# Eight feed-forward gate products as seven block products each

## The chip, the cores and the metric

The kernel runs on one core of a Trainium2 chip. TensorE (PE) multiplies, VectorE (DVE) and ScalarE (ACT) work on tiles in SBUF and PSUM, GpSimd (POOL) and SyncE (SP) issue transfers here. The metric is the device time of one execution in microseconds (us); lower is better. A matmul or tile shape such as 128x512 is partitions by elements.

## The reference

One decoder layer on x (256 tokens, 2048 wide), everything in f32:

```
h = swiglu(rms_norm(x), wg1, wu1, wd1);   x = x + 0.5 * rms_norm(h)
m = hybrid_mixer(rms_norm(x), mem, ...);  x = x + rms_norm(m)
h = swiglu(rms_norm(x), wg2, wu2, wd2);   out = x + 0.5 * rms_norm(h)
swiglu(u) = (silu(u @ wg) * (u @ wu)) @ wd        wg, wu: 2048 x 5504
```

The mixer projects u, runs a gated recurrence, a forgetting attention and an attention over a memory (mem_kv = rms_norm(mem) @ w_mem_kv, which needs nothing of x), gates the three and multiplies by w_o. Every norm has its gains.

## The kernel before, in words

**Products in halves.** Each f32 operand is split exactly into a high and a low part of 12 bits (`split`: the copy on ScalarE, L164, then the subtraction on VectorE, L165), and a product is three matmuls into the same sum: high by high (L278), high by low (L279), low by high (L281). The weights are the moving operand, 512 columns at a time; the input, transposed, is the stationary one, 128 x 128.

**Weights.** `Weights` loads the k tiles (128 rows) of up to 1024 columns: a raw tile of 1 MB (two k tiles, `N_RAW` 3) comes on SP's queue, and each k tile is split into a pair whi, wlo of 1024 wide (`N_SPLIT` 6 pairs).

**`linear`** walks over k in batches and lets the two token tiles t = 0, 1 of 128 tokens alternate within a batch; `head` and `tail` are the lengths of the first and the last batch. Its callbacks take what is in PSUM: `evac` per token tile, `by_chunk` after each 512 columns. `before` runs ahead of a batch. Work that needs TensorE in between (transposes) is put off by a batch (`soon`, `tasks`). PSUM has 5 banks for sums and 3 for transposes.

**`ffn`.** d_ff is 43 tiles of 128, in parts of 16, 16 and 11. In a part, each eight tiles make a gate group (16 k tiles x 2 token tiles x 2 chunks x 3 = 192 matmuls; silu at L391 on ScalarE) and an up group (192 matmuls; L396 on VectorE multiplies by the gate), then hT is transposed and split. Behind a part comes its down product; its sum is kept in SBUF tiles y.

**`closer`** ends a sub-layer: y is multiplied by the gains (L343), normalised with the residual added (L360, on VectorE, token tile by token tile), transposed into the next input (L171, L182, L183) and stored. The row scale rstd of that input is applied later, where sums leave PSUM.

**Order.** Every engine has an in-order queue, which the Tile scheduler sets from its own model of times; buffers come from pools (`slot` 21, `tmp` 7), so an operation also waits for a free buffer. Memory keys and values are made behind the first feed-forward; the transposes of the memory stand among the batches of its last down product. At the start x is loaded, transposed and split ahead of the batches of the first gate group.

```
for f in range(f0, f1, 8):                     # in each of the three parts
    linear(from_uT(u), Weights(KD, chunks(wg)), evac_gate)
    linear(from_uT(u), Weights(KD, chunks(wu)), evac_up)
```

Of the kernel before, what the change touches and what calls it, by code (L numbers as in the profile page):

```python
# [9 lines left out]
F32 = mybir.dt.float32  # L10
# [17 lines left out]
N_SLOT = 21  # L28
N_TMP = 7
N_RAW = 3  # L30
N_SPLIT = 6
N_ACC = 5
N_TP = 3
BIG = 6


def constants():
    """Identity, causal bias and the level masks: they depend on shapes alone."""
# [15 lines left out]
def layer(ctx: ExitStack, tc: tile.TileContext, a, out: bass.AP):  # L54
# [22 lines left out]

    def acc(w):
        return psp.tile([P, 512], F32, tag="acc", bufs=N_ACC, name=nm("acc"))[:, :w]

    def tp(*shape):
        n = int(np.prod(shape))
        t = psp.tile([P, 512], F32, tag="tp", bufs=N_TP, name=nm("tp"))[:, :n]
        if len(shape) == 2:
            t = t.rearrange("p (a b) -> p a b", b=shape[1])
        return t
# [12 lines left out]
    def columns(rows, q):  # L99
        """Vectors [1, n * 128] as n columns each, found by col()."""  # L100
# [16 lines left out]
    turn_first = columns([("ffn1_pre", 16)], S)  # L117
    turn_rest = columns([("mem_norm", 16), ("mix_pre", 16), ("ffn2_pre", 16), ("hgrn_lb", 12), ("hgrn_gnorm", 6)], G)
# [35 lines left out]
    def touch(func, src):  # L154
        """Has the table of func loaded by the time src is there."""
# [6 lines left out]
    def split(hi, lo, src):  # L162
        """hi + lo = src exactly, 12 bits each."""
# [3 lines left out]
    def transposed(src, n):  # L167
        """n blocks of [P, 128] of src, each transposed, in PSUM."""
# [5 lines left out]
    def split_T(hi, lo, src, n, gain=None):  # L174
        """hi, lo: [P, n, 128] slices for src^T (times gain per row)."""
# [10 lines left out]
    class Weights:  # L186
# [3 lines left out]
        def __init__(self, nk, chunks, kb=None, early=0):  # L190
# [6 lines left out]
            self.kb = kb or max(1, 2048 // self.width)  # L197
# [6 lines left out]
        def load(self, n):  # L204
            width, k0 = self.width, len(self.parts)
            raw = pool.tile([P, 2048], F32, tag="raw", bufs=N_RAW, name=nm("raw"))[:, :n * width]
# [742 lines left out]
```

## Time and profile before

| | |
|---|---|
| device time, median of 3 runs | 2263.7 us (2262.32 to 2264.56) |
| span of the profiled execution | 2262.2 us |
| TensorE busy | 2243.5 us (99%), 10674 instructions |
| VectorE busy | 1245.6 us (55%) |
| ScalarE busy | 1048.0 us (46%) |
| loaded and stored | 434.33 MB, mean 192 GB/s |

The profile is of one execution, and its span lies 1.5 us below the median of the runs. Busy time is the time an engine spent in instructions; a row of a group gives the count, the busy time and the mean of one, then how long the engine was idle just before them and what ended that. The chain goes back from the last instruction to what each waited for.

### The profile page before, as it was taken

The page shows a single profiled execution, that of the slowest core. Times are in us where ns is not written, and L with a number is a line of the kernel's source. Part 1 is how long each engine was busy: PE and PEld are TensorE (multiplying, and loading weights), DVE is VectorE, ACT ScalarE, POOL GpSimd, SP SyncE. Part 2 cuts the span into 40 slices and gives each one's busy share as a digit, 9 for nine tenths or more (in the row PEclk, how much of TensorE's full clock was granted, in tenths as well). Part 3 has the DMA queues.
Part 4 walks back from the last instruction along what each step waited for, and adds up shares of the span by engine and source line. Part 5 has one row for each costly group of instructions (what it writes and reads, how often), then busy time and mean ns, then how long its engine had stood idle before and what let it go on. Part 6 is the DMA issues. An engine that isn't in the chain of part 4 may idle for free.

```text
span 2262.2 us, 26732 instructions
## 1 busy us (share of the span) xinstructions
PE 2243.5 (99%) x10674; PEld 1914.7 (85%) x10674; DVE 1245.6 (55%) x1519; ACT 1048.0 (46%) x1351; POOL 33.1 (1%) x61
## 2 busy tenths in 40 slices
PE   9999999999999999999999999999999999999998
PEld 7888888888898799999888888888888888888896
DVE  5545445454456856686555545557545445455455
ACT  6444444443446744445444444446444444443443
POOL 0000000000000000000000000000000000000000
PEclk9999999999999999999999999999999999999999
DMA  8555565557555644546656566665656555557553
GB/s 267 187 191 189 178 206 187 201 172 258 188 182 197 224 154 154 166 151 176 194 179 199 187 197 216 217 208 188 203 187 186 187 202 186 186 192 255 179 184 121
DMA packets 138540, 434.33 MB, mean 192 GB/s; under 512 B 9080, under 2 KB 42064, under 8 KB 138416
## 3 DMA queue, kind: packets, MB, share of 16 engines
q1 hardware_dynamic: 133568, 417.41, 55.6%
q0 software_dynamic: 4672, 15.15, 2.4%
q8 instruction: 83, 1.36, 0.2%
q14 instruction: 41, 0.34, 0.0%
q10 hardware_dynamic: 176, 0.07, 0.0%
HBM read 426.30 MB, written 6.30 MB: 191 GB/s over the span
## 4 chain that ended last, share of the span: by engine, by line
PE 97%; DMA 1%; DVE 1%; ACT 0%; SPq 0%; issue 0%; DVEq 0%; ACTq 0%
PE acc L278 31%; PE acc L279 31%; PE acc L281 31%; PE tp L171 2%; PE tp L671 1%; DMA x<-in_x_dram 0%; DMA raw<-in_ffn_wu_dram 0%; DMA x<-in_mem_dram 0%; DVE y L360 0%; DVE wlo L165 0%; ACT whi L164 0%; PE tp L584 0%; PE tp L600 0%; ACT junk L160 0%; PE tp L665 0%; PE tp L818 0%
## 5 line engine op out<-in xcount | busy, mean ns | idle before, releaser
L165 DVE TENSOR_TENSOR wlo<-raw,whi 128x1024 fp32r<-128x1024 f32 (+2 forms) x818 | 958.5, 1177 | 866.0 <-ACT whi L164 829.1
L164 ACT ACTIVATE whi<-raw 128x1024 fp32r<-128x1024 f32 (+2 forms) x818 | 833.2, 1024 | 1006.6 <-PE acc L281 956.4
L278 PE MATMUL acc<-whi,uh 128*128 128x512 f32 (+1 forms) x2264 | 856.6, 379 | 1.6 <-ACT uh L182 1.5
L279 PE MATMUL acc<-wlo,uh 128*128 128x512 f32 (+1 forms) x2264 | 849.2, 376 | 0.8 <-DVE wlo L165 0.8
L281 PE MATMUL acc<-whi,ul 128*128 128x512 f32 (+1 forms) x2264 | 670.2, 376 | 0.1
L278 PEld LDWEIGHTS acc<-whi,uh 128*128 128x128 f32 x2264 | 425.0, 188 | 68.2 <-ACT uh L182 3.0
L279 PEld LDWEIGHTS acc<-wlo,uh 128*128 128x128 f32 x2264 | 425.2, 188 | 66.5 <-DVE wlo L165 1.3
L281 PEld LDWEIGHTS acc<-whi,ul 128*128 128x128 f32 x2264 | 421.1, 188 | 66.6 <-DVE ul L183 0.5
L278 PE MATMUL acc<-whi,hh 128*128 128x512 f32 x688 | 269.2, 391 | 0.0
L279 PE MATMUL acc<-wlo,hh 128*128 128x512 f32 x688 | 268.0, 390 | 0.0
L281 PE MATMUL acc<-whi,hl 128*128 128x512 f32 x688 | 228.4, 389 | 0.0
L281 PEld LDWEIGHTS acc<-whi,hl 128*128 128x128 f32 x688 | 129.1, 188 | 26.9
L278 PEld LDWEIGHTS acc<-whi,hh 128*128 128x128 f32 x688 | 129.2, 188 | 26.5
L279 PEld LDWEIGHTS acc<-wlo,hh 128*128 128x128 f32 x688 | 129.2, 188 | 26.3
L396 DVE SCALAR_TENSOR_TENSOR sg<-acc,rstd,sg 128x512 f32<-128x512 f32 (+1 forms) x44 | 31.2, 733 | 34.3 <-PE acc L281 29.9
L278 PE MATMUL acc<-whi,eh 128*128 128x512 f32 x128 | 50.1, 391 | 0.0
L279 PE MATMUL acc<-wlo,eh 128*128 128x512 f32 x128 | 49.8, 389 | 0.0
L391 ACT ACTIVATE sg<-acc,rstd 128x512 f32<-128x512 f32 (+1 forms) x44 | 27.7, 677 | 44.0 <-PE acc L281 43.3
L281 PE MATMUL acc<-whi,el 128*128 128x512 f32 x128 | 42.9, 391 | 0.0
L183 DVE SCALAR_TENSOR_TENSOR ul<-tp,vec,uh 128x128 fp32r<-128x128 f32 x96 | 29.6, 345 | 7.3 <-ACT uh L182 7.0
L182 ACT ACTIVATE uh<-tp,vec 128x128 fp32r<-128x128 f32 x96 | 31.1, 380 | 5.5 <-DVE ul L183 4.2
L281 PEld LDWEIGHTS acc<-whi,el 128*128 128x128 f32 x128 | 24.0, 188 | 5.0
(262 smaller groups left out, 1097.1 us busy)
## 6 DMA issues: line engine op xcount, KB each, us to landing
raw<-in_ffn_wd_dram SPq DMA_DIRECT2D x84, 1024.0 KB, 5.4
raw<-in_ffn_wu_dram SPq DMA_DIRECT2D x80, 1024.0 KB, 4.9
raw<-in_ffn_wg_dram SPq DMA_DIRECT2D x72, 1024.0 KB, 4.9
raw<-in_w_gate_dram SPq DMA_DIRECT2D x48, 1024.0 KB, 5.2
raw<-in_w_in_dram SPq DMA_DIRECT2D x96, 384.0 KB, 3.7
raw<-in_w_o_dram SPq DMA_DIRECT2D x16, 1024.0 KB, 5.6
raw<-in_ffn_wg_dram SPq DMA_DIRECT2D x16, 512.0 KB, 4.7
raw<-in_w_mem_kv_dram SPq DMA_DIRECT2D x8, 1024.0 KB, 5.0
```

The source lines that it names most:

```text
L164: S.activation(hi, src, AF.Copy)
L165: V.tensor_tensor(lo, src, f32(hi), ALU.subtract)
L171: PE.transpose(p[:, i, :], src[:, i * P:(i + 1) * P], ident)
L182: S.activation(hi[:, i, :], p[:, i, :], AF.Copy, scale=g)
L183: V.scalar_tensor_tensor(lo[:, i, :], p[:, i, :], g, f32(hi[:, i, :]), ALU.mult, ALU.subtract)
L278: PE.matmul(ps[t][c], lh, wh[:, sl], start=(k == 0), stop=False)
L279: PE.matmul(ps[t][c], lh, wl[:, sl], start=False, stop=False)
L281: PE.matmul(ps[t][c], ll, wh[:, span[c]], start=False, stop=(k == nk - 1))
L391: S.activation(sg[t][:, i * 512:i * 512 + p.shape[-1]], p, AF.Silu, scale=r(t))
L396: V.scalar_tensor_tensor(h, p, r(t), h, ALU.mult, ALU.mult)
L671: PE.matmul(L[:, 2 * i + j, :], K[:, i, j * P:(j + 1) * P], Q[:, i, j * 64:(j + 1) * 64], start=True, stop=True)
```

## The change

- **Gate groups.** In each feed-forward the gate product of tiles 8 to 39 is made, per eight tiles, by `seven`: the input u (256 x 2048) and the weights (2048 x 1024) are seen as 2 x 2 blocks (A11, A12 are token tile 0 with k tiles 0 to 7 and 8 to 15, A21, A22 token tile 1; B is cut at row 1024 and column 512), and seven products of block sums give the four blocks of the result. Each product has 8 k tiles x 3 = 24 matmuls, so 168 for 192.
- **Sums of the input** (`new_forms`, once a feed-forward): four sums of A, 8 additions or subtractions and 4 splits, 1024 wide.
- **Sums of the weights**, per set of two k tiles (four sets a group, raw tiles x, y, e, h of 512 KB): T1 = B11 + B12 and T3 = B22 + B12 on VectorE (L388, L390). T2 = T1 + B22 and T4 = T2 + B21 (signs are in the forms) by `more`, a load on POOL's queue that adds what it brings into the raw tile (L378); in the last set these are on VectorE too (L393, L394, L399). Each set is split seven times, once per product.
- **Combining** the products: one ScalarE copy and seven 512-wide sums on VectorE out of PSUM.
- **Blocks.** The order in a feed-forward is, per block of eight tiles, gate, down of the block before, up; the down sums go by a ScalarE copy and a store on POOL's queue to DRAM (L603, from the second block on an adding store, L605) and come back at the end.
- **The rest.** Memory keys and values move to the very start; there x is loaded on POOL's queue, scaled by its own rstd on ScalarE, and transposed. The mixer's first projections are those of the recurrence. To keep scales apart, `closer` takes power-of-two scales. Pools: `slot` 28, `tmp` 5, 8 raw tiles of 512 KB, one pool of 8 PSUM banks.

```diff
-N_SLOT = 21
-N_TMP = 7
-N_RAW = 3
+N_SLOT = 28
+N_TMP = 5
+N_RAW = 8
 N_SPLIT = 6
-N_ACC = 5
-N_TP = 3
+N_BANK = 8
...
+    def new_forms(u):
...
+        forms = {1: a11, 2: a12, 4: a22}
+        whole(f[0], a22)
+        whole(f[1], a21)
+        V.tensor_tensor(f[0], f[0], f[1], ALU.subtract)
+        halves(5, f[0])
+        whole(f[2], a11)
+        V.tensor_tensor(f[1], f[2], f[1], ALU.subtract)
+        halves(7, f[1])
+        V.tensor_tensor(f[2], f[2], f[0], ALU.add)
+        halves(6, f[2])
+        whole(f[3], a12)
+        V.tensor_tensor(f[3], f[2], f[3], ALU.subtract)
+        halves(3, f[3])
...
+    def seven(forms, W, col, evac):
...
+        for s in range(n_set):
+            last = s == n_set - 1
+            order += [(7 * s + d, p, s) for d, p in ((0, 1), (1, 3), (2, 5), (3, 2))]
+            order += [(7 * s + d, p, s) for d, p in (((4, 6), (5, 7), (9, 4)) if last else ((4, 7), (8.5, 6), (14.5, 4)))]
+        order.sort()
...
+        def load(s):
+            r = []
+            for i, j in ((0, 0), (1, 1), (0, 1), (1, 0)):
+                x = raw_tile()
+                nc.sync.dma_start(out=x.rearrange("p (k c) -> p k c", c=512), in_=src(i, j, s))
...
+        def more(x, i, j, s):
+            G.dma_start(out=x.rearrange("p (k c) -> p k c", c=512), in_=src(i, j, s), accum_op=ALU.add)
+
+        for n, (_, p, s) in enumerate(order):
...
+            split(hi, lo, {1: x, 3: y, 5: x, 2: h, 7: y, 6: x, 4: x}[p])
+            if p == 1:
+                V.tensor_tensor(x, x, e, ALU.add)
+            elif p == 3 and not last:
+                V.tensor_tensor(y, y, e, ALU.add)
+            elif p == 5:
+                if last:
+                    V.tensor_tensor(x, x, y, ALU.add)
+                    V.tensor_tensor(y, y, e, ALU.add)
+                else:
+                    more(x, 1, 1, s)
+            elif p == 6:
+                if last:
+                    V.tensor_tensor(x, x, h, ALU.add)
+                else:
+                    more(x, 1, 0, s)
...
+            ah, al = forms[p]
+            for i in range(2):
+                k, ws = 2 * s + i, slice(512 * i, 512 * i + 512)
+                PE.matmul(bank[p], ah[:, k, :], hi[:, ws], start=(seen[p] == 0), stop=False)
+                PE.matmul(bank[p], ah[:, k, :], lo[:, ws], start=False, stop=False)
+                PE.matmul(bank[p], al[:, k, :], hi[:, ws], start=False, stop=(seen[p] == 7))
...
+                    x = tmp([P, 512], "part")
+                    S.activation(x, ps, AF.Copy)
+                    dst = ysum[t * P:(t + 1) * P, c * 512:(c + 1) * 512]
+                    if f0 == 0:
+                        G.dma_start(out=dst, in_=x)
                     else:
...
+                        G.dma_start(out=dst, in_=x, accum_op=ALU.add)
...
+        for f in range(0, last, BLOCK):
+            if f == 0:
+                linear(lu, first, gate_plain, head=head)
+            else:
+                if forms is None:
+                    forms = new_forms(u)
+                seven(forms, wg, f * P, gate_seven)
+                down(f - BLOCK, f)
+            linear(lu, Weights(KD, chunks(wu, f, BLOCK)), lambda t, ps, f=f: up(t, ps, f, BLOCK))
```

Three places show what moves. The first is VectorE's queue where, in the first feed-forward, the second gate group begins. Before, from the up group's multiplication on (sg; hl is the split of hT, wlo that of the weights):

```order
L396 SCALAR_TENSOR_TENSOR sg_566<-acc_593,rstd_478,sg_566 128x512
L165 TENSOR_TENSOR hl_848<-tp_849,hh_847 128x4x128
L165 TENSOR_TENSOR hl_857<-tp_858,hh_856 128x4x128
L396 SCALAR_TENSOR_TENSOR sg_566<-acc_594,rstd_478,sg_566 128x512
L165 TENSOR_TENSOR wlo_960<-raw_953,whi_959 128x1024
L165 TENSOR_TENSOR wlo_990<-raw_987,whi_989 128x1024
L165 TENSOR_TENSOR wlo_994<-raw_987,whi_993 128x1024
```

After, eight rows behind the last of these multiplications (form: sums of the input; sl: their low half; L390: a sum of the weights):

```order
L168 TENSOR_TENSOR wlo_1503<-raw_1485,whi_1502 128x1024
L168 TENSOR_TENSOR sl_1383<-form_1375,sh_1382 128x1024
L326 TENSOR_TENSOR form_1377<-uh_296,ul_297 128x1024
L390 TENSOR_TENSOR raw_1485<-raw_1485,raw_1487 128x1024
L339 TENSOR_TENSOR form_1376<-form_1377,form_1376 128x1024
L168 TENSOR_TENSOR wlo_1514<-raw_1403,whi_1513 128x1024
L341 TENSOR_TENSOR form_1377<-form_1377,form_1375 128x1024
L168 TENSOR_TENSOR sl_1389<-form_1376,sh_1388 128x1024
L168 TENSOR_TENSOR sl_1394<-form_1377,sh_1393 128x1024
L326 TENSOR_TENSOR form_1378<-uh_298,ul_299 128x1024
L344 TENSOR_TENSOR form_1378<-form_1377,form_1378 128x1024
L168 TENSOR_TENSOR sl_1400<-form_1378,sh_1399 128x1024
```

Before, only the next group's splits stand there. After, the operations of `new_forms` stand among them, nine of the twelve in these rows, and the split of the last form, sl_1400, which product 3 needs, comes last.

The second is VectorE's queue in the group after that, at its first products 6 and 4. raw_2403 is tile x of set 0 (into which POOL's queue adds ahead of each of the two reads), raw_2483 that of set 1, raw_2556 that of set 2:

```order
L168 TENSOR_TENSOR wlo_2514<-raw_2403,whi_2513 128x1024
L168 TENSOR_TENSOR wlo_2526<-raw_2483,whi_2525 128x1024
L168 TENSOR_TENSOR wlo_2537<-raw_2489,whi_2536 128x1024
L168 TENSOR_TENSOR wlo_2547<-raw_2485,whi_2546 128x1024
L168 TENSOR_TENSOR wlo_2565<-raw_2556,whi_2564 128x1024
L388 TENSOR_TENSOR raw_2556<-raw_2556,raw_2560 128x1024
L168 TENSOR_TENSOR wlo_2576<-raw_2403,whi_2575 128x1024
L168 TENSOR_TENSOR wlo_2587<-raw_2558,whi_2586 128x1024
```

Between product 6's split of raw_2403 and product 4's stand five operations; there is no such pair before, where a raw tile is loaded once and split once.

The third is TensorE's queue where w_o ends and the second feed-forward begins (el: the merged input; uh, ul: the next input; ym: the sub-layer's result). Before, at the end of w_o for t = 1, and 47 matmuls later:

```order
L278 MATMUL acc_11567<-whi_11742,eh_11082 128x512
L279 MATMUL acc_11567<-wlo_11743,eh_11082 128x512
L281 MATMUL acc_11567<-whi_11742,el_11083 128x512
L278 MATMUL acc_12056<-ehi_11748,uh_11224 128x512
L279 MATMUL acc_12056<-elo_11749,uh_11224 128x512
L278 MATMUL acc_12057<-ehi_11748,uh_11224 128x512
```

```order
L279 MATMUL acc_12057<-wlo_12139,uh_11224 128x512
L281 MATMUL acc_12056<-whi_12138,ul_11225 128x512
L171 MATMUL tp_11952<-ident,ym_11218 128x128 x4
L281 MATMUL acc_12057<-whi_12138,ul_11225 128x512
L171 MATMUL tp_11969<-ident,ym_11218 128x128 x4
L171 MATMUL tp_11986<-ident,ym_11219 128x128 x4
```

After, at the end of w_o for t = 1:

```order
L283 MATMUL acc_12541<-whi_12730,eh_11996 128x512
L284 MATMUL acc_12541<-wlo_12731,eh_11996 128x512
L286 MATMUL acc_12541<-whi_12730,el_11997 128x512
L174 MATMUL tp_12947<-ident,ym_12138 128x128 x4
L174 MATMUL tp_12964<-ident,ym_12138 128x128 x4
L174 MATMUL tp_12981<-ident,ym_12139 128x128 x4
L174 MATMUL tp_12998<-ident,ym_12139 128x128 x4
L283 MATMUL acc_13059<-ehi_12736,uh_12506 128x512
```

The transposes of t = 1 stood among the next group's products for t = 0, 47 matmuls in; now all sixteen stand ahead of the first of them. They stand so at the end of the first feed-forward too, where memory keys and values came next before.

## Rows read from the trace of the kernel before

**Rows 1.** The page, parts 1 and 4: busy time; the chain's shares by engine and line.

```profile
PE 2243.5 (99%) x10674; PEld 1914.7 (85%) x10674; DVE 1245.6 (55%) x1519; ACT 1048.0 (46%) x1351; POOL 33.1 (1%) x61
...
PE 97%; DMA 1%; DVE 1%; ACT 0%; SPq 0%; issue 0%; DVEq 0%; ACTq 0%
PE acc L278 31%; PE acc L279 31%; PE acc L281 31%; PE tp L171 2%; PE tp L671 1%; DMA x<-in_x_dram 0%; DMA raw<-in_ffn_wu_dram 0%; DMA x<-in_mem_dram 0%; DVE y L360 0%; DVE wlo L165 0%; ACT whi L164 0%; PE tp L584 0%; PE tp L600 0%; ACT junk
```

**Rows 2.** Windows over an up and the next gate group: busy us (count), clock, DMA.

```profile
core 0: us, PE busy (x) PEld busy (x) DVE busy (x) ACT busy (x) POOL busy (x), PEclk, DMA share, GB/s
109.50:155.00 45.50, 45.50 (x207) 37.79 (x205) 21.81 (x19) 21.39 (x23) 0.00 (x0) 1.00 0.59 196
155.00:198.40 43.40, 43.40 (x198) 36.00 (x197) 22.54 (x22) 16.94 (x18) 0.00 (x0) 1.00 0.55 182
```

**Rows 3.** The chain in order of time: start us, us, what.

```profile
103.17 0.87 PE tp L171 x8
...
192.03 0.87 PE tp L171 x8
```

**Rows 4.** Waits: engine and line, released by: total us, times, longest.

```profile
engine line waited for: us in total, times, longest us
...
ACT whi L164 <- PE acc L281: 956.4, 652, 7.8
DVE wlo L165 <- ACT whi L164: 829.1, 367, 7.6
```

**Rows 5.** Lines by form: busy us, mean ns of one, idle before and what ended it.

```profile
L165 DVE TENSOR_TENSOR wlo<-raw,whi 128x1024 fp32r<-128x1024 f32 x674 | 821.8, 1224 | 777.3 <-ACT whi L164 742.8
L164 ACT ACTIVATE whi<-raw 128x1024 fp32r<-128x1024 f32 x674 | 711.8, 1061 | 851.2 <-PE acc L281 822.6 <-issue 11.9 <-DMA raw<-in_ffn_wg_dram 9.1
...
L165 DVE TENSOR_TENSOR hl<-tp,hh 128x512 fp32r<-128x512 f32 x40 | 25.7, 683 | 0.0
```

**Rows 6.** VectorE's timeline at three places: start us, us, what, idle before.

```profile
236.46 4.63 DVE L165 TENSOR_TENSOR wlo<-raw,whi 128x1024 fp32r<-128x1024 f32 x4 [7.61 <-ACT whi L164]
...
1441.42 1.28 DVE L891 TENSOR_TENSOR merged<-merged,gm 128x512 f32<-128x512 f32 x2
...
1603.99 2.59 DVE L165 TENSOR_TENSOR wlo<-raw,whi 128x1024 fp32r<-128x1024 f32 x2 [2.85 <-ACT whi L164]
1609.43 2.59 DVE L165 TENSOR_TENSOR wlo<-raw,whi 128x1024 fp32r<-128x1024 f32 x2 [2.85 <-ACT whi L164]
```

**Rows 7.** The residual's POOL loads, tile xr; then issues, page part 6.

```profile
DMA to landing us min/median/max: 4.0/5.0/6.2
...
raw<-in_ffn_wg_dram SPq DMA_DIRECT2D x16, 512.0 KB, 4.7
```

**Rows 8.** TensorE's timeline where w_o ends and the second feed-forward begins.

```profile
1536.50 0.40 PE L281 MATMUL acc<-whi,el 128*128 128x512 f32 x1
1536.74 0.39 PE L278 MATMUL acc<-ehi,uh 128*128 128x512 f32 x1
...
1547.58 0.60 PE L171 MATMUL tp<-ident,ym 128*128 128x128 f32 x4
```

**Rows 9.** VectorE's timeline at the same place, the last split and normalising.

```profile
1545.32 1.21 DVE L165 TENSOR_TENSOR wlo<-raw,whi 128x1024 fp32r<-128x1024 f32 x1
1546.45 2.73 DVE L360 SCALAR_TENSOR_TENSOR ym<-ym,sm,xr 128x512 f32<-128x512 f32 x4
1549.10 0.60 DVE L183 SCALAR_TENSOR_TENSOR ul<-tp,vec,uh 128x128 fp32r<-128x128 f32 x2
```

**Rows 10.** Windows over the end, columns as in rows 2.

```profile
2250.00:2255.00 5.00, 1.16 (x6) 0.61 (x4) 3.56 (x11) 2.38 (x7) 0.00 (x0) 0.98 0.27 102
2255.00:2262.00 7.00, 0.00 (x0) 0.00 (x0) 2.40 (x3) 0.04 (x1) 1.73 (x1) 0.50 0.40 150
```

**Rows 11.** The same over the start, then the chain where the memory comes in.

```profile
0.00:40.00 40.00, 35.26 (x159) 27.99 (x160) 24.66 (x49) 28.23 (x57) 4.48 (x12) 1.00 0.84 273
...
760.40 0.62 ACT junk L160 x2
761.28 7.13 DMA x<-in_mem_dram
768.54 0.63 PE tp L171 x4
```

More of the change, by code (lines that the diff above doesn't have):

```diff
@@ L205, in load @@
             width, k0 = self.width, len(self.parts)
[L206 to L207 removed]
+            raw = raw_tile()[:, :n * width].rearrange("p (k c) -> p k c", c=width)
             off = 0
@@ new lines, in from_uT, with whole, halves @@
+    def from_uT(u):
+        return lambda k, t: tuple(x[:, k % 8, :] for x in u[t][k // 8])
+    def new_forms(u):
+        f = [slot([P, 1024], F32, "form") for _ in range(4)]
+        (a11, a12), (a21, a22) = u
+        def whole(dst, a):
+            V.tensor_tensor(dst, f32(a[0].rearrange("p k c -> p (k c)")), f32(a[1].rearrange("p k c -> p (k c)")), ALU.add)
+        def halves(name, src):
+            h, l = slot([P, 8, P], F32R, "sh"), slot([P, 8, P], F32R, "sl")
+            split(h.rearrange("p k c -> p (k c)"), l.rearrange("p k c -> p (k c)"), src)
+            forms[name] = (h, l)
+        forms = {1: a11, 2: a12, 4: a22}
[11 more added lines that the diff above has]
+        halves(3, f[3])
+        return forms
@@ L447, in ffn, with evac @@
+                def evac(t, ps, half=half):
+                    if close and half == 1:
+                        close[2](t)
                 rows = wd[f0 * P:f1 * P]
                 wts = Weights(f1 - f0, [(rows, half * 1024, 512), (rows, half * 1024 + 512, 512)])
-                linear(lambda k, t: tuple(h[:, k % 4, t, :] for h in hT[f0 + k - k % 4]), wts, evac2,
-                       tail=BIG if closing and not before_close else 4, by_chunk=by_chunk,
-                       before=before_close if closing else None)
@@ L452, in ffn @@
-        return un, rn
+                linear(lambda k, t: tuple(h[:, (f0 + k) % 4, t, :] for h in hT[(f0 + k) // 4 * 4]), wts, evac,
+                       tail=BIG if close and half else 4, by_chunk=by_chunk)
+        last = n_tile // BLOCK * BLOCK
+        for f in range(0, last, BLOCK):
+            if f == 0:
+                linear(lu, first, gate_plain, head=head)
+            else:
+                if forms is None:
[3 more added lines that the diff above has]
+            linear(lu, Weights(KD, chunks(wu, f, BLOCK)), lambda t, ps, f=f: up(t, ps, f, BLOCK))
@@ new lines, in both, with start @@
+        def both(t, ps):
+            gate_plain(t, ps[:1])
+            return up(t, ps[1:], last, n_tile - last)
+        linear(lu, Weights(KD, chunks(wg, last, n_tile - last) + chunks(wu, last, n_tile - last)), both)
+        y = [[slot([P, 1024], F32, "y") for _ in range(2)] for _ in range(2)]
+        begin, chunk, post, un, rn, sq, _ = closer(y, gpost, 0.5, resid, keep, gname, final, None, unscale)
+        def start(half):
+            for t in range(2):
+                G.dma_start(out=y[t][half], in_=ysum[t * P:(t + 1) * P, half * 1024:(half + 1) * 1024])
+            begin(half)
@@ L454, in layer @@
+        down(last - BLOCK, n_tile, (start, chunk, post))
+        return un, rn, sq
     W = {k: a[k][0] for k in ("ffn1_wg", "ffn1_wu", "ffn1_wd", "w_in", "w_mem_kv", "w_hgrn_out", "w_fox_out",
@@ L470, in pre_rstd @@
         V.tensor_reduce(s3, s2, AX.X, ALU.add)
-        r = pool.tile([P, 1], F32, tag="rstd", bufs=16, name=nm("rstd"))
+        r = keep_small()
         V.tensor_copy(r, rsqrt(s3, D))
         return r
-    s_x = [small([P, 4], "ss2") for _ in range(2)]
-    r0 = {}
-    u0 = new_uT()
     wp = tp(P)
```

332 lines of the change are left out of this document (199 added, 133 removed).

## The prediction

> **What bounds the kernel now.** I read the page first: TensorE is busy 99% of the span, and the chain that ended last is TensorE for 97% of it, almost all in the three product lines L278, L279 and L281 [rows 1]. Next the windows over one up group and the gate group after it, to see whether that average hides anything: TensorE fills all of both, at full clock, while VectorE and ScalarE are about half busy [rows 2]. The chain then gives the price of a matmul: the same eight transposes close two successive blocks of eight tiles at 103.17 and 192.03 [rows 3], 88.86 us for 384 matmuls and 16 transposes. Two rows of eight transposes are 0.87 us each, so a matmul costs (88.86 - 1.74) / 384 = 0.2269 us, and a gate group of 192 with its share of the transposes about 45.3 us. The waits say who follows whom: ScalarE's split waits 956 us for TensorE to give a split pair back, VectorE 829 us for ScalarE [rows 4]. So TensorE is the pace, and the splits run as far ahead as six pairs allow. Fewer matmuls are worth their full price only while the splits can still keep up; that is the whole question here.
>
> **What VectorE can do.** The mean of a 1024-wide subtraction is 1.22 us and of ScalarE's copy 1.06 us [rows 5], but neighbours overlap: four subtractions in a row take 4.63 us [rows 6], so one more costs (4.63 - 1.22) / 3 = 1.14 us. Two 512-wide sums take 1.28 us; at 0.68 us for one (the 512-wide row in [rows 5]), the second costs 0.60. In a steady stretch VectorE does two splits (2.59 us) in each 5.44 us and idles 2.85 [rows 6].
>
> **Eight gate groups, TensorE's side.** 8 products of blocks become 7: 168 matmuls for 192, in eight groups, so 192 in all (the order has 7920 512-wide matmuls for 8112). At 0.2269 us that is -43.6 us, -5.4 a group, if TensorE stays the pace.
>
> **Six later groups, VectorE's side.** A group now asks 28 splits of 1024 and 10 sums of 1024 of VectorE, where before it asked 16 splits. How much of that can be done early? T is the end of the up group's last matmul. Six pairs, one of them still in use, let 5 splits go ahead, and with them 2 sums; they are done by about T+1. Left are 23 splits and 8 sums, 31 x 1.14 = 35.3 us, and about 12 short operations (what is left of the up group, and the combining of products), 12 x 0.60 = 7.2: T+43.5. TensorE's last product still runs after the last split, about 5 matmuls or 1.1 us: T+44.7, against 45.3 now. Without any further wait a group gains 0.6 us instead of 5.4. TensorE's own 38.1 us no longer decide.
>
> **The accumulating loads.** T2 and T4 of the first three sets are added into the raw tile by a load that POOL issues. T4's load can start when product 6's split has read the tile, and product 4's split of that tile comes five 1024-wide operations later on VectorE's queue (the change, second place): 5 x 1.14 = 5.7 us, less ScalarE's copy (1.06) and some 0.2 for hand-overs: 4.4 us for the load to hide. For product 6 of the set six operations stand between; the last set's are on VectorE. What is queued behind a late load is everything: ScalarE's and VectorE's queues are in order, and TensorE lives on them. Two such places a group lie past the lead (T4 of sets 0 and 1; they overlap the T2 loads, and T4 of set 2 has seven operations of cover). POOL's 512 KB loads took 4.0 to 6.2 us from issue to landing, median 5.0 here and 5.2 in another stage [rows 7]. They only write; the new ones also read their destination, and 2 MB a set come in on SP's queue beside them. No accumulating load is in the trace, so the bounds are wide: 4.0 (no wait) and, with destination traffic doubling the time past the shortest, 8 or so. I take 6.0, near the longest row: 2 x (6.0 - 4.4) = 3.2 us a group. A later group is then -0.6 + 3.2 = +2.6, six of them +15.6 (at 4.4 or less: -3.6; at 8: +39.6).
>
> The Trainium skill, "DMA: Bandwidth & Descriptors", section "Anatomy of one DMA — SWDGE (gpsimd) path", gives a load on this path as about 2.0 us plus its bytes over 436 GB/s, an estimate of 3.2 us for 512 KB. By that no landing would be late and the sum would be about 22 us lower. The trace disagrees for plain loads of that size, 4.0 us at the least and 5.0 in the median, so I go by the rows.
>
> **The first group of each feed-forward.** It also builds the forms of the input: 12 operations of 1024 on VectorE, 13.7 us, in its in-order queue between the splits (first place). If VectorE only gets longer by that, the group is at 44.7 + 13.7 = 58.4, +13.1. But product 3, third on TensorE's queue after two parts of product 1, needs the last form, and its split stands behind all others: two multiplications and two splits of hT to about T+2.8, 17 wide operations of 1.14 us and ScalarE's copy ahead of the last, so T+24. TensorE has done the 12 matmuls that stand before it by about T+8 (their second split is itself behind two forms) and then holds the pairs; VectorE cannot go on for long after. If nothing useful were done until T+24 the group would end 24 + 44.7 - 45.3 = +23.4. I take the middle, 18.2, and one late load (1.6; here only T4 of set 1 has five operations of cover): +19.8, two groups +39.6.
>
> **The two stage boundaries.** At the end of the feed-forward and of w_o, TensorE now goes into the next stage's products while VectorE normalises token tile 1. The last product of w_o for t=1 starts at 1536.50, the next stage's first at 1536.74, and t=1's transposes only at 1547.58 [rows 8]; VectorE's normalising ends by 1549.18 behind six splits [rows 9]. In the changed order these 16 transposes stand directly behind w_o's last product (third place), so TensorE waits for VectorE: to about 1549.7 instead of running through, 12.8 us, less the transposes themselves 1.74: 11 us. The same pattern stands where the first feed-forward ends, since memory keys and values, which filled that gap, are now at the start; fewer splits are in the way, about 10. +21 (0 if VectorE's chain comes without the six splits and quickly; 26 if a clock drop joins).
>
> **The clock.** In this trace TensorE is granted full clock (1.00) as long as it works, and 0.50, the 1.2 GHz level, in the last 7 us, after it has stopped [rows 10]. Four stalls of over 10 us (two forms, two boundaries) could each leave TensorE slow for a stretch after. How long it stays slow, and what a matmul costs then, no row shows; if it costs twice, 2 us a stall stand for some nine matmuls at that price (an estimate from 0.2269). I take 2 us each, +8, between 0 and 16.
>
> **Start and the rest.** Keys and values come first: their wait at 760 us for the memory input (TensorE idle about 1.8 us) goes, and a first load, 0 to 40 us, is filled with ScalarE and VectorE work at 0.7 and 0.6 [rows 11]; the scaling of x and its squares add to it, with ScalarE 28 of 40 us busy. I take 0 between -5 and +8. The down products' partial sums go out by ScalarE copies and POOL stores in place of VectorE sums: 0, covered by TensorE at 45 us per down of 8 tiles and by the up group that follows; if ScalarE (46% busy) had to wait for a store, its splits would be late by that. Smaller weight loads (512 KB took 4.7 us to land, [rows 7]) with eight buffers in place of three of 1 MB: 0.
>
> **Sum.** The trace's span is 2262.2 us; the median of the runs, 2263.7, lies 1.5 above it. 15.6 + 39.6 + 21 + 8 + 0 = +84.2: 2262.2 + 84.2 + 1.5 = 2348 us, 3.7% slower. Its own range: 2320 to 2390.
>
> **Rivals.**
> - The loads land in time and the first groups only grow by their 12 operations: -3.6 + 26.2 + 21 + 8 = +52, 2315; with the boundaries at 10 and the clock at 2, 2298. For it: 4.0 us is in the rows [rows 7]. Against: the median is over the 4.4 us, and those loads only write. 2290 to 2320, chance 0.17.
> - The accumulating loads take 8 us or more: 39.6 + 2 x (18.2 + 3.6) + 21 + 8 = +112, 2376; at 10 us +140, 2404. For it: reading and writing the same 512 KB, beside the weight stream. Against: the DMA engines are half idle (share 0.55 to 0.59, [rows 2]). Over 2375, chance 0.16.
> - The other side, faster: TensorE stays the pace. If VectorE's 31 wide operations after T cost under 0.9 us each, or its lead were nine or ten splits, not five, the groups give their -43.6, and with forms hidden the boundaries (+21) and the clock (+8) leave -15: 2249, and 2230 if the boundaries cost little. Decided at VectorE's work of 39 us past T. For it: VectorE idles half of the up group before [rows 6]. Against: six pairs are all it may fill there, and the pitch of 1.14 is measured. 0.08.
> - Gains and waits cancel to within 0.2% (about what a measurement of this kernel can tell from no change), 2259 to 2268: 0.03.
>
> The forecast itself, VectorE as the pace with landing waits and two boundary stalls, has 0.56. Slower by over 0.2% sums to 0.89, faster to 0.08, no change to 0.03. The range leaves out the fast case and the far end of the slow loads: 2290 to 2395.
>
> **What would show it.** In a later seven-product group: VectorE without idle time, TensorE waiting for the subtraction of the split and the group's length near 48 us; short gaps on ScalarE that end with a load of the gate weights on POOL's queue, and that queue's time to landing (6 forecast). In the first such group: a TensorE gap of over 10 us ending with the last form's split. At both boundaries: a TensorE gap of about 10 us just ahead of transposes of y. In the page: VectorE up by 200 x 1.14 = 230 us or so, TensorE's busy time down by about 40. Wrong would be: TensorE full in the seven-product groups, or a load time that has no gap behind it, or a first group no longer than a later one.

## The result, and the profile after

The changed kernel takes 2408.99 us (median of 4 runs, 2405.07 to 2411.74) against 2264.13 for the kernel before: 6.4% slower, ratio 1.0637 with a 95% interval of 1.0622 to 1.0652. The forecast was 2348 us, the range 2290 to 2395. The direction was right and the size was not: +145 us where +84 had been summed.

The profiled execution has a span of 2403.3 us. Of the page, the busy times and the adding loads (the last number is the median from issue to landing):

```profile
PE 2251.8 (94%) x10482; PEld 1890.4 (79%) x10482; DVE 1489.1 (62%) x1781; ACT 1190.2 (50%) x1533; POOL 148.2 (6%) x185
...
raw<-in_ffn_wg_dram POOLq DMA_DIRECT2D x48, 512.0 KB, 7.0
```

TensorE is busy for as long as before [rows 1], where about 40 us less had been forecast for 192 matmuls of 512 fewer: 15 us of that are matmuls at half clock (below), and short waits between two matmuls count partly as busy. By the single records, from the start of one matmul to the start of the next, what goes beyond the usual distance for the shape sums to 198 us, 14 before; 15 and 1 of that are the matmuls at half clock. 184 more, less the 43.6 for 192 matmuls, is 140 of the 141 us by which the span grew. VectorE has gained 244 us.

The windows over a later group (the second of the first feed-forward) and over a first one, columns as in [rows 2]:

```profile
core 0: us, PE busy (x) PEld busy (x) DVE busy (x) ACT busy (x) POOL busy (x), PEclk, DMA share, GB/s
315.20:371.20 56.00, 45.44 (x183) 33.30 (x182) 44.95 (x46) 31.46 (x36) 6.08 (x5) 0.97 0.74 188
160.50:227.50 67.00, 44.87 (x180) 33.72 (x179) 56.31 (x54) 33.65 (x37) 6.00 (x5) 0.85 0.60 154
```

Before, a gate group was 45.3 us long with its share of the transposes, all TensorE [rows 2], [rows 3]. From the first to the last of its products a later group now takes 53.8 to 57.7 us (six of them, 331.7 together), a first one 66.8 and 67.1. VectorE is busy for 45 of the 56 us: it has most of the work, but it also waits, and that was the part to explain. The next timeline is ScalarE's in that later group, with the idle time ahead of a row and what ended it in brackets:

```profile
320.16 1.06 ACT L167 ACTIVATE whi<-raw 128x1024 fp32r<-128x1024 f32 x1 [2.15 <-DMA raw<-in_ffn_wg_dram]
...
331.71 2.00 ACT L167 ACTIVATE whi<-raw 128x1024 fp32r<-128x1024 f32 x2 [5.43 <-DMA raw<-in_ffn_wg_dram]
337.79 2.95 ACT L167 ACTIVATE whi<-raw 128x1024 fp32r<-128x1024 f32 x3 [4.07 <-DMA raw<-in_ffn_wg_dram]
...
348.06 2.00 ACT L167 ACTIVATE whi<-raw 128x1024 fp32r<-128x1024 f32 x2 [4.70 <-DMA raw<-in_ffn_wg_dram]
353.43 2.00 ACT L167 ACTIVATE whi<-raw 128x1024 fp32r<-128x1024 f32 x2 [3.37 <-DMA raw<-in_ffn_wg_dram]
```

Five times in this group (four to six times in the six later ones, 17 to 22 us) ScalarE stands still for a load of gate weights, 19.7 us in all, and all of these are adding loads, three for T2 and two for T4; before, ScalarE's splits waited 956 us for TensorE [rows 4] and 9.1 for loads of gate weights [rows 5]. The loads themselves are issued here (POOL's timeline of the same group; the second row is two loads), and below it the landing times of all 48, where the plain POOL loads before took 4.0, 5.0 and 6.2 [rows 7]:

```profile
313.23 1.23 POOL L378 DMA_DIRECT2D raw<-in_ffn_wg_dram  x1 [39.88 <-DVE wlo L168]
325.87 2.47 POOL L378 DMA_DIRECT2D raw<-in_ffn_wg_dram  x2 [11.40 <-ACT whi L167]
340.41 1.20 POOL L378 DMA_DIRECT2D raw<-in_ffn_wg_dram  x1 [12.07 <-DVE wlo L168]
342.68 1.20 POOL L378 DMA_DIRECT2D raw<-in_ffn_wg_dram  x1 [1.07 <-DVE wlo L168]
356.05 1.20 POOL L378 DMA_DIRECT2D raw<-in_ffn_wg_dram  x1 [12.17 <-DVE wlo L168]
```

```profile
DMA to landing us min/median/max: 5.6/7.0/11.3
```

By the single records, the two loads issued at 325.87 and 326.73 land at 331.61 and 337.69, after 5.7 and 11.0 us. In every later group the first of such a pair takes 5.7 to 8.3 us and the second 10.2 to 11.3.

In a first group TensorE waits twice for the forms, for the second split of product 1 and then for product 3:

```profile
166.74 0.50 PE L409 MATMUL acc<-wlo,uh 128*128 128x512 f32 x1 [4.41 <-DVE wlo L168]
...
182.79 0.79 PE L408 MATMUL acc<-whi,sh 128*128 128x512 f32 x1 [14.07 <-ACT sh L167]
```

And at the two boundaries; at the second, [rows 8] had the next stage's product 0.24 us behind w_o's last one:

```profile
853.55 2.82 PE L174 MATMUL tp<-ident,y 128*128 128x128 f32 x12 [10.08 <-DVE y L522]
```

```profile
1622.04 3.33 PE L174 MATMUL tp<-ident,ym 128*128 128x128 f32 x16 [10.35 <-DVE ym L522]
```

The windows over the first form wait, the first boundary and what follows each show the clock (the column behind the last count), 0.50 and 0.62 just after:

```profile
170.00:182.80 12.80, 0.01 (x1) 0.01 (x1) 11.64 (x12) 3.17 (x3) 1.22 (x1) 0.50 0.39 82
182.80:187.00 4.20, 4.16 (x9) 2.86 (x10) 1.20 (x1) 0.84 (x1) 0.00 (x0) 0.50 0.00 0
843.50:853.50 10.00, 0.00 (x0) 0.00 (x0) 9.89 (x28) 6.21 (x14) 0.00 (x0) 0.66 0.48 138
853.50:858.00 4.50, 4.45 (x22) 4.46 (x23) 3.88 (x12) 4.48 (x16) 2.16 (x4) 0.62 1.04 388
```

There TensorE starts again at the lower level, 1.2 GHz: from 182.79 its 512-wide matmuls stand 0.43 us apart, not 0.227. 76 matmuls of the run stand so far apart, which costs 15.1 us (before, 4 and 0.8).

### The profile page after: what moved, and what is told of

The parts are those of the page before. It is cut to its first block, busy times and chain, and to the rows that moved or that the text cites. A ratio compares the mean times of both kernels' runs of the same rounds, so it can differ in the third digit from the quotient of the medians.

```text
span 2403.3 us, 28497 instructions
## 1 busy us (share of the span) xinstructions
PE 2251.8 (94%) x10482; PEld 1890.4 (79%) x10482; DVE 1489.1 (62%) x1781; ACT 1190.2 (50%) x1533; POOL 148.2 (6%) x185
## 5 line engine op out<-in xcount | busy, mean ns | idle before, releaser
L168 DVE TENSOR_TENSOR wlo<-raw,whi 128x1024 fp32r<-128x1024 f32 (+2 forms) x914 | 1061.8, 1180 | 776.6 <-ACT whi L167 747.8
L283 PE MATMUL acc<-whi,uh 128*128 128x512 f32 (+1 forms) x1752 | 656.6, 375 | 0.0
L284 PE MATMUL acc<-wlo,uh 128*128 128x512 f32 (+1 forms) x1752 | 650.7, 371 | 0.0
L286 PE MATMUL acc<-whi,ul 128*128 128x512 f32 (+1 forms) x1752 | 512.2, 371 | 0.0
L283 PEld LDWEIGHTS acc<-whi,uh 128*128 128x128 f32 x1752 | 329.1, 188 | 45.8 <-ACT mv L707 0.3
L284 PEld LDWEIGHTS acc<-wlo,uh 128*128 128x128 f32 x1752 | 329.2, 188 | 45.4
L286 PEld LDWEIGHTS acc<-whi,ul 128*128 128x128 f32 x1752 | 324.9, 188 | 46.2
L408 PE MATMUL acc<-whi,sh 128*128 128x512 f32 x256 | 108.6, 424 | 49.6 <-ACT sh L167 27.6
L409 PE MATMUL acc<-wlo,sh 128*128 128x512 f32 x256 | 110.4, 431 | 23.3 <-DVE wlo L168 23.1
L378 POOL DMA_DIRECT2D raw<-in_ffn_wg_dram x48 | 58.3, 1251 | 796.8 <-DVE wlo L168 714.1
L410 PE MATMUL acc<-whi,sl 128*128 128x512 f32 x256 | 105.9, 414 | 0.1
```

The source lines that it names most:

```text
L168: V.tensor_tensor(lo, src, f32(hi), ALU.subtract)
L283: PE.matmul(ps[t][c], lh, wh[:, sl], start=(k == 0), stop=False)
L284: PE.matmul(ps[t][c], lh, wl[:, sl], start=False, stop=False)
L286: PE.matmul(ps[t][c], ll, wh[:, span[c]], start=False, stop=(k == nk - 1))
L378: G.dma_start(out=x.rearrange("p (k c) -> p k c", c=512), in_=src(i, j, s), accum_op=ALU.add)
L408: PE.matmul(bank[p], ah[:, k, :], hi[:, ws], start=(seen[p] == 0), stop=False)
```

## Experiments

The theory after the result: VectorE's pace leaves a later group at about 44 us, and the adding loads, late for ScalarE, make it 54 to 58. The rival: VectorE, or the six pairs, make it that long anyway. The runs e1, e2 and e5 tell these apart, e3, e4 and e12 price the boundaries and the rest of the change, e6 the forms, e7 to e11 try another engine for the sums, and e13 to e15 count VectorE's operations. "Groups" are the eight seven-product groups, from first to last matmul.

**e1, e2, e5: the adding loads.** e1 and e5 leave out `more` for both sums and for T4; e2 keeps it without the addition.

```diff
-                    more(x, 1, 1, s)     # e1: both are left out; e5: only the one below
+                    pass
...
-                    more(x, 1, 0, s)
+                    pass
...
-            G.dma_start(out=x.rearrange("p (k c) -> p k c", c=512), in_=src(i, j, s), accum_op=ALU.add)   # e2
+            G.dma_start(out=x.rearrange("p (k c) -> p k c", c=512), in_=src(i, j, s))
```

> Left out: the 48 adding loads of the sets 0 to 2 (T2 and T4 are then not formed there); nothing else changes. Theory: the later groups last 54 to 58 us because ScalarE waits for these loads (about 18 us a group, loads of 5.6 to 11.3 us). Without them a later group should fall to VectorE's pace, about 45 to 46 us (-10 each, six of them), and a first group by 3 to 5 us: 2409 - 60 - 8, about 2340 us. Rival: VectorE's 28 splits and 10 sums set the length anyway and the waits for loads only lie beside them: groups stay above 52 us, the time above 2395.

Measured: 2323.12 us, ratio to before 1.0257 (1.0242 to 1.0273). The six later groups take 44.1 to 44.3 us, the first ones 61.4 and 62.0. The window over a later group:

```profile
core 0: us, PE busy (x) PEld busy (x) DVE busy (x) ACT busy (x) POOL busy (x), PEclk, DMA share, GB/s
311.90:356.20 44.30, 40.90 (x183) 32.85 (x181) 44.22 (x46) 31.82 (x36) 0.00 (x0) 1.00 0.54 166
```

VectorE is busy for 44.22 of 44.30 us. That is the pace of 23 splits and 8 sums that the prediction had worked out (44.7). The theory holds; the gain of 86 us is 18 more than expected: 6 of that lie in the later groups (11 us each, not 10), 3 in the first ones; the rest was not taken apart. Matmuls at half clock fall from 76 to 39 (15.1 to 7.6 us), inside the groups and behind them.

> The 48 loads stay on POOL's queue with the same bytes and the same waits, but overwrite the tile in place of adding to it (T2 and T4 are wrong then). If the adding itself makes them slow (reading the destination too), they should land in 4.5 to 5.5 us as the other POOL loads did before, two in flight should not stretch to 11, and most of the first run's gain should come: about 2350 to 2365 us. If POOL's queue is what is slow, whatever the load does, landing stays at about 7 us and the time within 10 us of 2409.

Measured: 2338.12 us, ratio 1.0325 (1.0309 to 1.034); later groups 43.5 to 46.9 us. Landing of the 48 loads, now plain:

```profile
DMA to landing us min/median/max: 3.9/4.3/6.9
```

4.3 us in the median against 7.0: with the same bytes, queue and waits it is the adding that makes them late. 71 of the 86 us come back, and the time is 12 us under the range expected.

> Left out: the second adding load of each set 0 to 2 (B21, T4 is then T2); the first one stays, so 24 adding loads in place of 48 and never two in flight together. Theory: one adding load alone takes 5.6 to 5.9 us and it is the pair that stretches to 7.5 and 10.5; alone it is hidden behind six or more operations (6.8 us less 1.3), late by 0 to 1 us each. A later group then ends at 44.5 to 47 us (44.2 without any, 53.8 to 57.7 with both), the time at 2325 to 2345 us. Rival: each adding load costs its share whether or not another is in flight: half of the 86 us, about 2365 us.

Measured: 2378.84 us, ratio 1.0509 (1.0494 to 1.0525), a miss. Without a second one in flight the loads still take long, and ScalarE waits for each:

```profile
DMA to landing us min/median/max: 5.5/7.6/10.3
```

```profile
320.26 1.06 ACT L167 ACTIVATE whi<-raw 128x1024 fp32r<-128x1024 f32 x1 [1.90 <-DMA raw<-in_ffn_wg_dram]
...
334.16 2.95 ACT L167 ACTIVATE whi<-raw 128x1024 fp32r<-128x1024 f32 x3 [5.36 <-DMA raw<-in_ffn_wg_dram]
...
349.40 2.00 ACT L167 ACTIVATE whi<-raw 128x1024 fp32r<-128x1024 f32 x2 [7.77 <-DMA raw<-in_ffn_wg_dram]
```

Groups are 50.6 to 54.9 us. So the pair in flight is not the whole reason. In the records the load issued at 339.05, which lands after 10.2 us, has three loads of down weights (512 KB each, SP's queue) issued between 339.92 and 343.32 beside it, and these take 5.2 to 8.4 us. All eight groups repeat it: the third adding load, with three loads of down weights issued within 4.3 us behind it, takes 9.0 to 10.3 us. The second takes 7.2 to 8.8 with three loads of gate weights behind it (later groups), but 5.5 and 6.0 with two that come later (first groups). Plain loads lengthen too where many are in flight. The median of these eight in the changed kernel was 5.2 us before; four of them now follow the loads of the down sums at once and land after 13.7 to 16.2 us:

```profile
xr<-x POOLq DMA_DIRECT2D x8, 512.0 KB, 11.2
```

So what moves beside an adding load, its twin or the weights, seems to make it later; this is read from these patterns and was not tried by itself. Why it is slower than a plain one beside the same traffic (e2) stays open.

**e3, e4, e12: boundaries and the rest.** e3 gives PSUM two pools again (5 banks for sums, 3 for transposes), e4 makes all gate groups plain in the changed kernel, e12 does both.

```diff
-        t = psp.tile([P, 512], F32, tag="bank", bufs=N_BANK, name=nm("tp"))[:, :n]
+        t = psp.tile([P, 512], F32, tag="tp", bufs=N_TP, name=nm("tp"))[:, :n]
...
-                bank[p] = acc(512)
+                bank[p] = tp(512) if p in (6, 4) else acc(512)
```

> The whole computation; PSUM is again 5 banks for sums and 3 for transposes (products 6 and 4 of a group take two of the 3). Theory on the boundaries: with one pool the scheduler put the 16 transposes of the second token tile ahead of the next stage; with two pools the next stage's products stand ahead of them, as before, and both gaps of 10.2 and 10.5 us go: 2409 - 20 = 2389 us, with the groups as they were. Rival: the gap only moves (TensorE waits in the next stage for splits or for the input): 2405 to 2412. The group may pay for fewer free banks: then above 2412.

Measured: 2382.78 us, ratio 1.052 (1.0505 to 1.0536), 26 us less than the changed kernel. Neither boundary gap is left; the longest there is this one:

```profile
841.15 0.62 PE L285 MATMUL acc<-wlo,uh 128*128 128x384 f32 x2 [1.49 <-DVE wlo L169]
```

The order of TensorE's queue follows from the pools: with two, the next stage's products stand ahead of the second token tile's transposes again. By the records TensorE's gaps at the two boundaries fall by 17 us and not by 20; 6 more come from its first 70 us (gaps of 11.6 us with one pool, 5.2 with two, 4.3 before the change) and 6 from the first groups (63.5 and 64.2), while a new gap of 2.6 stands in the mixer (at 1117 us).

> The changed kernel with all gate groups plain again (192 matmuls, no sums, no adding loads, no forms of the input): what is left of the change is the order in blocks, the down sums through DRAM, memory keys and values first, one PSUM pool. Theory: it pays for the two boundaries (21 us), a slow clock behind them (some 3 us) and a slower start (5 to 8 us), and nothing else: 2264 + 30, about 2294 us; so the seven-product groups carry the other 115 of the 145 us. Rival: the down sums through DRAM and the smaller loads cost by themselves: above 2310 us.

Measured: 2295.43 us, ratio 1.0138 (1.0121 to 1.0155). As expected: the two boundary gaps are there (10.09 and 10.35 us), and without seven products the change costs 31 us. The other 114 us are the seven-product groups.

> e4 (all gate groups plain) with two PSUM pools: the whole computation. Theory: e4's 31 us over the kernel before are the two boundaries with the slow clock behind them (24 to 26 us, as in e3) and the start (5 to 7): 2269 to 2273 us. Rival: the blocks, the down sums through DRAM or the smaller loads cost by themselves: above 2280 us.

Measured: 2276.0 us, ratio 1.0053 (1.0038 to 1.0068), between the two. The second pool takes 19 of e4's 31 us: TensorE's gaps shrink by 17 us at the boundaries and by 4 in the first 70 us, and one of 3.4 appears in the mixer (at 1066 us). Of the gaps in what is left, 12 us over the kernel before, 7.0 us lie in the first 70 us, 2.8 at the first boundary (about 783 us) and 3.4 that one in the mixer, against 4.3 us in the first 70 and 1.6 at the memory input before; the rest was not followed up.

**e6: the forms.** `new_forms` is called ahead of block 0's up group.

```diff
                 linear(lu, first, gate_plain, head=head)
+                forms = new_forms(u)
             else:
...
```

> The whole computation; the forms of the input are built during the up group of block 0, not behind it. Theory: in the first seven-product group of each feed-forward 12 VectorE operations stood ahead of product 3's last split and TensorE waited 14.2 and 4.6 us there; with the forms ready the group is like a later one: 66.8 and 67.1 us become 54 to 57, so 2409 - 22, about 2387 us. Rival: the forms' 13.7 us of VectorE are not hidden in the up group (its splits get late) and most of it comes back there: above 2398 us.

Measured: 2381.53 us, ratio 1.0524 (1.0509 to 1.054): 27 us less. The first groups take 55.3 and 54.7 us, like later ones, and the first of them starts at 160.5 us as before this edit: VectorE's half-idle up group hides the forms.

**e7 to e11: the sums on GpSimd.** e7 makes T2, T3 and T4 of the sets 0 to 2 there; e9 only T2 and T4, with T3 summed into e by VectorE; e10 is e9 with two pools and early forms, e11 adds T3 to it; e8 is e7 with both.

```diff
...
+            elif p == 3:
+                V.tensor_tensor(e, e, y, ALU.add)            # e9, e10; e7: T3 (y, y, e) stands behind T2 below
             elif p == 5:
...
+                (V if last else G).tensor_tensor(x, x, y, ALU.add)
             elif p == 6:
...
+                (V if last else G).tensor_tensor(x, x, h, ALU.add)
```

> The whole computation; in the sets 0 to 2 the sums T2, T3 and T4 are made by GpSimd from the raw tiles in SBUF (9 operations of 128x1024 a group), no adding loads. Estimate from the 1.74 us of a 128x512 sum on GpSimd before: 3.5 us each, 31 us a group, the one between product 6's and product 4's split just hidden. If VectorE keeps its 1.14 us beside it, a later group is paced by 23 splits and 4 sums (31 us) and the short ones (7): about TensorE's own 38 to 42 us, eight groups together some 100 us less than with adding loads: about 2300 us. Rival: GpSimd and VectorE slow each other (VectorE's 1.22 us a split grows beside a GpSimd sum), or GpSimd takes over 4.4 us a sum and its in-order queue makes T4 late: groups of 46 us or more, above 2330 us.

> The whole computation with two PSUM pools, early forms and the sums of the sets 0 to 2 on GpSimd. If the three gains add up: 26 (pools, measured), 20 (forms) and 100 (sums) off 2409, about 2263 us, level with the kernel before; a little lower if the groups, with the other waits gone, reach TensorE's 38 us (8 x 45.3 - 8 x 39 = 50 us below the kernel with plain gates in blocks and without boundary gaps, 2275): 2225 to 2265 us. Rival: GpSimd's sums disturb VectorE: 2290 us or more.

Measured: e7 2487.85 us (ratio 1.0991, 1.0973 to 1.1009), e8 2432.84 (1.0746, 1.073 to 1.0762), both misses; groups of 63 us, in e7 the first ones 80. GpSimd's and ScalarE's timelines of e7:

```profile
342.26 3.25 POOL L394 TENSOR_TENSOR raw<-raw,raw 128x1024 f32<-128x1024 f32 x1 [9.42 <-issue]
345.48 3.35 POOL L391 TENSOR_TENSOR raw<-raw,raw 128x1024 f32<-128x1024 f32 x1
348.90 2.34 POOL L392 TENSOR_TENSOR raw<-raw,raw 128x1024 f32<-128x1024 f32 x1
```

```profile
332.88 1.06 ACT L167 ACTIVATE whi<-raw 128x1024 fp32r<-128x1024 f32 x1 [6.02 <-POOL raw L392]
...
351.28 4.84 ACT L167 ACTIVATE whi<-raw 128x1024 fp32r<-128x1024 f32 x5 [10.52 <-POOL raw L392]
...
368.57 4.84 ACT L167 ACTIVATE whi<-raw 128x1024 fp32r<-128x1024 f32 x5 [9.45 <-POOL raw L392]
```

T4 of a set (L394), T2 (L391) and T3 (L392) of the next follow one another on GpSimd, and ScalarE waits 6 to 10.5 us for their last: my edit had put T3, which product 7 reads at once, behind the others.

> The whole computation. T3 is summed into tile e by VectorE, so that B22 stays in y; T2 and T4 of the sets 0 to 2 are then single GpSimd sums (6 a group) where e7 made three in a row and product 7 waited behind two of them. Measured in e7: 2.4 to 3.5 us a sum, against 4.4 us of cover and 5.6 to 11.3 us for an adding load. Theory (late sums are what lengthens a later group, whoever makes them): groups of 44 to 47 us, near the 44.2 without any second sums, and the time at 2325 to 2345 us. Rival (GpSimd's sums hold VectorE up; in e7 some splits beside one took 2.6 to 3.4 us instead of 1.22): 50 us and more a group, above 2370 us.

Measured: 2424.45 us, ratio 1.0709 (1.0691 to 1.0727), a miss; later groups of 54.9 us, the first ones 73.7 and 73.9. A sum had not taken 2.4 to 3.5 us in e7, as expected here, but up to 5.6. GpSimd's sums, then two of VectorE's rows at the same time:

```profile
334.53 6.65 POOL L394 TENSOR_TENSOR raw<-raw,raw 128x1024 f32<-128x1024 f32 x1 [11.62 <-ACT whi L167]
341.14 2.35 POOL L392 TENSOR_TENSOR raw<-raw,raw 128x1024 f32<-128x1024 f32 x1
349.43 3.30 POOL L394 TENSOR_TENSOR raw<-raw,raw 128x1024 f32<-128x1024 f32 x1 [5.93 <-DVE wlo L168]
352.69 3.36 POOL L392 TENSOR_TENSOR raw<-raw,raw 128x1024 f32<-128x1024 f32 x1
```

```profile
333.18 5.75 DVE L168 TENSOR_TENSOR wlo<-raw,whi 128x1024 fp32r<-128x1024 f32 x5
...
348.13 11.28 DVE L168 TENSOR_TENSOR wlo<-raw,whi 128x1024 fp32r<-128x1024 f32 x6
```

A sum takes 2.35 us when VectorE leaves GpSimd alone and up to 6.65 when not; VectorE's six splits take 11.28 us where 1.22 + 5 x 1.14 = 6.9 were due. They hold each other up. The Trainium skill, "SBUF — State Buffer", section "Who interferes with whom", has this as a rule: a VectorE instruction with two inputs in SBUF contends with a GpSimd instruction that reads SBUF, since its second input comes through a read interface that the two share, under an exclusive lock. The rows agree in both directions: the sum of 6.65 us has five splits beside it, and two of the six splits take 3.4 us each while a sum runs.

> e9 with two PSUM pools and early forms, the whole computation. If the gains add (26 and 27 us, each measured alone), 53 us under e9: about 2280 us for groups of 45 us, that is the 45.3 of a plain gate group and no gain from seven products; 2265 to 2295. Rival: with the first groups and boundaries mended the rest shows what they covered (loads of weights, GpSimd): 2300 or more.

> e10 with T3 of the sets 0 to 2 on GpSimd as well (9 sums a group) and product 7 half a place later. VectorE has three sums less in a group: if its pace is the limit, 3 x 1.14 = 3.4 us a group less, 8 groups 27 us: about 2250 us, under the kernel before (2264). If GpSimd's sums come late for product 7, or slow VectorE, no gain or a loss: 2280 to 2330 us.

Measured: e10 2367.88 us (ratio 1.0456, 1.044 to 1.0471), 57 under e9, so the gains of pools and forms add up (53 expected), but on groups of 54.9 us where the 2280 had rested on 45. e11 2378.3 (1.0503, 1.0487 to 1.0519), over both of its ranges, groups of 56.3: taking three more sums off VectorE makes it slower. The second group of e10, then of e11, columns as in [rows 2]:

```profile
300.30:355.40 55.10, 44.59 (x181) 32.81 (x180) 51.12 (x45) 29.86 (x34) 21.27 (x6) 0.97 0.41 139
301.20:357.90 56.70, 43.30 (x182) 32.14 (x181) 55.51 (x43) 30.00 (x34) 24.65 (x8) 1.00 0.41 138
```

With two operations fewer in the window VectorE is busy for 4.4 us more: GpSimd holds it up for longer than it relieves it.

**e13, e14, e15: VectorE's count.** All three have two pools and early forms. e13 makes every sum on VectorE (T3 into e), e14 leaves T2 and T4 of the sets 0 to 2 out, e15 all sums of the weights.

```diff
...
             elif p == 5:                                     # e13; e15: no branch of this kind
...
+                V.tensor_tensor(x, x, y, ALU.add)
             elif p == 6:
...
+                V.tensor_tensor(x, x, h, ALU.add)
```

> The whole computation; two PSUM pools, early forms, and all four sums of the weights in every set on VectorE (T3 into tile e), no adding loads and no GpSimd sums. If VectorE's pace sets the length and nothing else, six sums more than in e1 cost 6 x 1.14 = 6.8 us on its 44.2: groups of 51 us, all eight alike, and 2276 (e12, plain groups of 45.3) + 8 x 5.7 = 2322 us. If the group has another limit near 54 us (pairs, loads), 2345 or more.

> Two PSUM pools and early forms; left out: T2 and T4 of the sets 0 to 2 (no adding loads, no sums for them). The floor of this design if second sums were free: groups of 44.2 us as in e1, first ones too: 2276 - 8 x 1.1 = 2267 us, no gain over the kernel before. If e1's other waits had covered something, 2280 or more; if the groups fall further once the first groups are mended, under 2255.

> Two PSUM pools and early forms; left out: all sums of the weights (28 splits a group stay on VectorE). VectorE's pace would be 44.2 - 8 x 1.14 = 35 us, under TensorE's 168 x 0.2269 = 38.1 and 1.7 of transposes. If VectorE was the limit, TensorE now is: groups of 39 to 40 us, 2276 - 8 x 5.5 = 2232 us, the whole price of the 192 matmuls. If splits alone (28 against 16) or their six pairs are the limit, groups stay at 42 us or more, 2250 us or more.

Measured: e13 2318.63 us (ratio 1.0239, 1.0224 to 1.0255), e14 2268.07 (1.0015, 1.0006 to 1.0025), e15 2232.75 (0.9857, 0.9841 to 0.9873); groups of 48.8 to 49.4, 44.1 to 44.3 and 38.9 us, in each all eight alike. The window over the second group of e13, e14 and e15:

```profile
294.60:343.60 49.00, 42.51 (x181) 32.09 (x180) 48.95 (x50) 29.55 (x33) 0.00 (x0) 1.00 0.49 153
```

```profile
287.40:331.80 44.40, 40.99 (x184) 32.92 (x182) 44.32 (x46) 31.78 (x36) 0.00 (x0) 1.00 0.54 166
```

```profile
283.10:322.20 39.10, 39.10 (x180) 32.49 (x178) 36.77 (x37) 31.95 (x34) 0.00 (x0) 1.00 0.62 198
```

VectorE fills the whole group in e13 and e14 (48.95 of 49.0, 44.32 of 44.4 us) and TensorE waits; in e15 TensorE fills it (39.10 of 39.1) and VectorE no longer does. So the length is VectorE's work until that falls under TensorE's 39 us; the pairs and the plain loads set no floor of their own above that. e13's groups are 2 us shorter than the 51 expected, six more sums cost 4.7 us in them and not 6.8. But from the start of the second group to that of the third it is 137.7 us, 131.4 in e14: 6.3 more, of which a wait of TensorE behind the group's last product is part (1.1 us, up to 345.25). Eight times 6.3 is the 51 us between the two runs, so the sums cost nearly their full price.

e15 is under the kernel before, but without the sums; none of the runs that make the whole computation is. The nearest, e12, has no seven products in it.

## Why the prediction was wrong

- **TensorE's side**: right. At TensorE's pace eight groups gain 43 us (e12 to e15), -5.4 each as summed.
- **VectorE's pace in a later group**: right. T+44.7 was worked out, 44.1 to 44.3 measured (e1, e14). In the changed kernel itself VectorE is not without idle time, as the forecast had it for a group near 48 us, but busy for 45 of 56 us.
- **The accumulating loads**: this step failed. It took two late places a group, T4 of the sets 0 and 1, because T2's loads would overlap them, and 6.0 us a load: 3.2 us a group. ScalarE waits at four to six places, for T2 as for T4, and a load takes 5.6 to 11.3 us, median 7.0. By the forecast's own reckoning T2's cover, six operations, is 5.6 us (6 x 1.14 less 1.06 and 0.2), already under the 6.0 it took, and it put these waits at nothing. The last load of a later group, with a single load of SP's issued over 4 us behind it, was near my 6.0 (5.6 to 5.9); that a second one in flight, or SP's loads, would make it later I had set aside, since the DMA share of 0.55 to 0.59 [rows 2] looked half idle. A later group lost 11 us to this (54 to 58 for 44.2), not 3.2: six groups are +60 where +15.6 stood, and with what a first group lost the whole step is worth 86 us (e1), of which 22 had been summed.
- **My upper end was too low as well**: 8 us a load gave +39.6 because only two places were counted; the rival of slow loads, over 2375 with a chance of 0.16, holds the time, but not for its reason alone: the median load took 7.0 us, not 8 or more, and the late places were more than two.
- **The first groups**: right in mechanism, +21.7 each for +19.8, and in size partly by luck: without the adding loads they are +16.4 (e1) where 18.2 stood for the forms, and the loads took 5.3 where 1.6 stood. e6 gets 27 us back by moving the forms alone.
- **The boundaries**: right in mechanism and size, 10.1 and 10.4 us for 10 and 11. What I had not named is the cause of the order, the one pool of PSUM banks (e3).
- **The clock**: 14 us more than before for +8, near the upper end (0 to 16). The stalls in later groups bring it down too: in e1 it is 7.6.
- **Start**: 0 was summed, between -5 and +8. TensorE's gaps in the first 70 us are 11.6 us, 4.3 before, so it came near the upper end; 6 of the 7 us more go with two pools (e3). e12 leaves 12 us over the kernel before for it and all else that is neither a group nor the order at the boundaries.
- **The 3.2 us for 512 KB** worked out from the Trainium skill, "DMA: Bandwidth & Descriptors", section "Anatomy of one DMA — SWDGE (gpsimd) path": neither plain loads (3.9 to 6.9 us, e2) nor adding ones (5.6 to 11.3) came down to it. The rows were the better guide, and still too low.

## What to carry to other kernels

When a change takes work off the bounding engine and gives it to another, count that engine's operations in the stretch itself and ask how many can be done ahead; here 31 operations of 1.14 us took all but 1 of the 5.4 us a group before any wait for a late sum (e14 against e12). A load that feeds a step a few microseconds later is to be priced with what else is in flight at that moment, not by the median of undisturbed loads. And buffers pooled together let the scheduler change an order far away: check it at the stage boundaries.

## What was not expected of the hardware

- An adding load of 512 KB needs 7.0 us in the median where a plain one on the same queue needs 4.3, and POOL is busy 1.2 us issuing it (records of e2: 0.72 for a plain one).
- A GpSimd sum of 128x1024 takes 2.35 us alone and up to 6.65 beside VectorE's subtractions, and six of those take 11.28 us in place of 6.9.
- After the stall of 14 us in the first group the granted clock was 0.50, the 1.2 GHz level, for the next 4.2 us; after that of 10 us at the first boundary it was 0.62 in the mean of 4.5 us.
